# Attention scores over all 128 rows, and the grouped-query keys of x and ctx in one tile

## The chip, the cores and the metric

The kernel runs on one core of one Trainium2 chip. The metric is the device time of one launch in microseconds (us), of which the median of three runs is quoted. TensorE is the engine of the matrix products (PE in the profile, its weight loads PEld), VectorE is DVE, ScalarE is ACT, GpSimd is POOL, and SyncE is SP.

## What is computed

A block with a retention and a recurrent branch is followed by two layers of a second block, all in float32. Each of the two layers mixes three branches: an mLSTM, a grouped-query attention ("gqa") and a neighbourhood attention ("na"). There are 256 tokens of x and 256 tokens of ctx. What matters here are the scores of the two attentions, heads of 64 features each:

```
def attend(q, k, v):                                  # gqa; softmax over all keys
    s = jnp.einsum('bqkgd,bskd->bkgqs', q, k).astype(jnp.float32) * (HEAD_DIM ** -0.5)
    p = jax.nn.softmax(s, axis=-1).astype(v.dtype)
    return jnp.einsum('bkgqs,bskd->bqkgd', p, v)
...
        s_win = jnp.einsum('bqhd,brqjhd->bhqrj', q_row, k_win).astype(jnp.float32) * scale + bias.astype(jnp.float32)
        s_ctx = jnp.einsum('bqhd,bshd->bhqs', q_row, kc).astype(jnp.float32) * scale
        s = jnp.concatenate([s_win.reshape(B, H, GRID_W, wr * wc), s_ctx], axis=-1)
        p = jax.nn.softmax(s, axis=-1).astype(v.dtype)
```

The queries of x see the keys of ctx and of x (512 keys). The queries of ctx, which only the first layer needs, see the keys of ctx alone (256 keys). gqa has 8 query heads on 2 key heads, na has 8 heads.

## The kernel before, in words

**Exact products from two parts.** Every operand of a large product is held as two float32r parts, a high one and a low one (the remainder). `mm3` (lines 120 to 125) makes a product out of three matmuls: high by high, high by low, low by high. These are the lines L123, L124 and L125 in the profile, and nearly all of TensorE's work is there: 128 rows of the contraction, 256 or 512 columns a matmul.

**Scores.** A head has 64 features, so its high and its low part fit one above the other on the 128 partitions. For a query head the tile `aqT` (gqa) or `nq` (na) holds the high part on partitions 0 to 63 and the low part on 64 to 127. For a key head there are two tiles: `akh` (`nkh` in na) holds the high part twice, on both halves; `akl` (`nkl`) holds the low part on partitions 0 to 63 alone. A score is two matmuls into one PSUM bank (a "unit" below has one bank of scores). The first contracts all 128 rows: query high and low with key high. The second contracts 64 rows: query high with key low. These are the lines L838 (gqa) and L925 (na). In gqa the keys of ctx and of x are separate tiles, so a unit of an x query has four matmuls of 256 columns; a unit of ctx queries also has four, two for each of its two tiles of 128 queries. In na the keys of ctx and x lie in one tile, and a unit of x has two matmuls of 512 columns, a unit of ctx four of 256.

**Counts.** A pair is two query heads. Each layer's gqa has four pairs, and each pair has 2 heads times 2 query tiles, so 16 units of x; the first layer has 8 units of ctx beside them. na has the same numbers of units.

**What runs around the scores.** `attend` (from line 629) writes one unit's scores, then lets `fill` trace independent TensorE work (gates L123 to L125, pieces of the modulation L339), then P @ V of a closed pair (L692), then the transposes of the unit two before (L678, L674). The softmax of a unit is VectorE's maximum (L657 or L648), ScalarE's exponential (L659 or L651) and VectorE's scaling (L661 or L653). In na, VectorE also adds the bias to the scores (L928). The list of independent work and the microseconds that are filled in stand in the code; they don't depend on what the change touches. The order on each engine is then made by a scheduler from that trace, and every engine runs its own list in order.

**Making the keys.** gqa: `keys` splits the normed keys token-major in the tile `hs` (high twice on ScalarE L771, low once on VectorE L772), transposes them (L781) and copies them to `akh` and `akl` (L783, L784). This runs once per sequence, at the start of gqa. na: `prepare` makes the queries and keys of one pair with products that are themselves part of the filled-in work, and splits the keys straight out of the PSUM bank `pk`: for each of two heads, ScalarE copies the high part twice (L896) and VectorE subtracts once (L897). It runs four times a layer, one pair ahead of its use, but for the first pair, whose scores wait for it.

**Weights.** Each chunk of 512 KB is loaded by SP into one of four `wr` tiles, cast by ScalarE (L106) and split by VectorE (L107).

Of the kernel before, what the change touches and what calls it, by code (L numbers as in the profile page):

```python
# [23 lines left out]
# microseconds of other TensorE work to trace ahead of the scores of gqa, with each of its units of  # L24
# scores and with each mLSTM head
FILLS = [(8.0, 3.6, 5.0), (4.0, 3.1, 2.5)]
# pieces of the last modulation kept for the gaps of the last layer; of them, those with tiles of their
# own in the layer's pool and in that of its output projection
TAIL, STOCK, STOCK_OUT = 24, 6, 5
# as many of its first pieces for the gap behind the first layer's output projection  # L30
# [30 lines left out]
class Work:  # L61
    """Independent TensorE work: gen(load()) is a generator that traces a piece and yields its microseconds."""
# [10 lines left out]
class Kern:  # L73
# [25 lines left out]
    def weights(self, src, eng=None, into=None):  # L99
        """A chunk [128, n] of weights as two exact float32r parts."""  # L100
# [9 lines left out]
    def split(self, hi, lo, src, scale=None):  # L110
        """hi + lo = src (* scale) as two float32r parts"""
# [8 lines left out]
    def mm3(self, ps, a, b, first, last):  # L120
        """ps (+)= a.T @ b with a, b = (high, low) parts"""
        mm = self.nc.tensor.matmul
        mm(ps, a[0], b[0], start=first, stop=False)  # L123
        mm(ps, a[0], b[1], start=False, stop=False)  # L124
        mm(ps, a[1], b[0], start=False, stop=last)  # L125

    def gemm_pieces(self, w, x, c0, c1, kts=KT, off=0):
        """Feature-major [128 outputs, tokens c0:c1] in pieces; weights stationary."""
# [18 lines left out]
    def gemm_tok(self, src, x, seqs, order=None, eng=None, among=None):  # L147
        """Token-major [128 tokens, 2 tiles, <=256] for each sequence; weights move, four k-tiles a chunk.
        among: (n, f) calls f ahead of the products of the n-th chunk from the end"""
# [19 lines left out]
    def gemm_last(self, src, x):  # L169
        """gemm_tok for one sequence and up to 24 k-tiles, one token tile [128, 256] after the other"""  # L170
# [15 lines left out]
    def step(self):  # L186
        """trace one piece of the independent work that is ready; False where there is none"""
# [17 lines left out]
    def fill(self, us):  # L205
        """trace independent TensorE work of about so many microseconds"""
# [8 lines left out]
    def require(self, works):  # L215
        """trace these pieces of work now, but for those already traced"""
# [6 lines left out]
    def rstd(self, pool, out, ss, n):  # L223
        """out = (ss / n + eps) ** -0.5 by Newton's iteration; its sign changes with each step, and starts negative"""
# [19 lines left out]
    def norm_scale(self, x, pool, ys, junk=None):  # L244
        """ys = rms-normed x, two token tiles; ys may be x where junk is given"""
# [10 lines left out]
    def norm_put(self, ys, temp, hi, lo, c0, gain, shift=None):  # L256
        """hi + lo [128, 8, c0:c0+256] = gain * ys (+ shift), feature-major"""
# [28 lines left out]
    def tanh2(self, out, src):  # L286
        """out = tanh(src / 2) = 2 sigmoid(src) - 1"""
        self.nc.scalar.activation(out, src, AF.Tanh, scale=0.5)

# [17 lines left out]
    def cond(self):  # L307
        """silu of the conditioning vectors, feature-major"""
# [11 lines left out]
    def modulation(self, l, pool=None):  # L320
        """silu(c) @ w_mod + b"""
# [29 lines left out]
    def stock(self, works, pool, n, y=False):  # L351
        """takes n pieces of modulation out of works; tiles of their own (or of the branches' outputs) for their weights"""
# [9 lines left out]
    def fetch(self, works):  # L362
        """their loads behind the last chunk of weights"""
# [5 lines left out]
    def mod_end(self, l, m, row):  # L369
        """one of the six vectors feature-major; gains (1 + scale) g of the norms; rows gate * g of the residual branches to DRAM"""  # L370
# [30 lines left out]
    def first_block(self):  # L401
        nc, A, tc = self.nc, self.A, self.tc
        with ExitStack() as es:
            pa = es.enter_context(tc.tile_pool(name="fa", bufs=1))
            # the parts of both halves of the mixed sequence; before, the LRU's states and ctx
# [5 lines left out]
            # -8 softplus(-lambda) and its half  # L411
# [19 lines left out]
            with tc.issue_after(put):  # L431
                self.cond()
                # half gate biases
# [999 lines left out]
```

## Time and profile before

| | us |
|---|---|
| median of 3 runs | 1889.11 |
| lowest and highest run | 1887.61, 1892.03 |
| profiled execution: span from first to last instruction | 1885.2 |
| PE busy in it | 1816.7 |
| DVE busy in it | 1152.7 |
| ACT busy in it | 861.4 |
| POOL busy in it | 252.9 |

The profile page has no time of the profiled execution but its span; the median run is 3.9 us above it. "Busy" is the time in which at least one instruction of the engine is in progress. The matmuls are pipelined: a matmul that lasts 0.39 us can be followed by the next one after 0.23 us, so what a matmul costs is read from the distance of two starts, not from its duration.

### The profile page before, as it was taken

To read this page: it belongs to the slowest core of one execution; us is meant where nothing else is said; L and a number is where in the kernel's file an instruction comes from. 1 tells how busy PE (TensorE), PEld (TensorE's weight loads), DVE (VectorE), ACT (ScalarE), POOL (GpSimd) and SP (SyncE) were. 2 spreads that over 40 slices of the span, in tenths; PEclk is the share of its full clock that TensorE was granted. 3 is DMA by queue.
4 is the path that set the end of the run, shared out by engine and by line. 5 is a ranking of instruction groups with operands and counts; after the bars stand their busy time and mean duration, and the time that the engine had idled before them with its cause. 6 is when DMAs were issued, how large, how long until landed. Compare 5 with 4: busy or idle time off the path is not lost.

```text
span 1885.2 us, 31900 instructions
## 1 busy us (share of the span) xinstructions
PE 1816.7 (96%) x12484; PEld 1595.4 (85%) x12484; DVE 1152.7 (61%) x2280; ACT 861.4 (46%) x1620; POOL 252.9 (13%) x182
## 2 busy tenths in 40 slices
PE   7998988999999999998999999998999999999998
PEld 6897987666898977787877889998889998779998
DVE  7878768444434667556655564239654448768874
ACT  5463344334435544434444443235555545446653
POOL 2214052000101021004111110021001011002210
PEclk9998998999999999999999999999999999999999
DMA  8853443555524342374354233344444744676563
GB/s 301 282 195 113 138 167 106 184 182 176 193 92 149 88 126 84 101 249 165 113 178 157 96 103 112 107 136 161 151 140 134 239 129 132 196 248 212 185 209 120
DMA packets 114422, 299.33 MB, mean 159 GB/s; under 512 B 28480, under 2 KB 41088, under 8 KB 114016
## 3 DMA queue, kind: packets, MB, share of 16 engines
q1 hardware_dynamic: 113568, 296.37, 47.9%
q8 instruction: 98, 1.61, 0.3%
q0 software_dynamic: 272, 0.36, 0.1%
q10 hardware_dynamic: 432, 0.57, 0.1%
q14 instruction: 52, 0.43, 0.1%
HBM read 281.46 MB, written 19.46 MB: 160 GB/s over the span
## 4 chain that ended last, share of the span: by engine, by line
PE 76%; DVE 6%; ACT 1%; issue 1%; DMA 0%; POOL 0%; DVEq 0%; ACTq 0%; POOLq 0%
PE psg L123 21%; PE psg L124 21%; PE psg L125 20%; PE pss L838 2%; PE psg L692 2%; PE psg L339 2%; PE pst L678 2%; PE pss L925 2%; PE pst L1054 1%; DVE wl L107 1%; PE pss L1042 1%; DVE rstd L240 1%; PE pst L264 0%; ACT wh L106 0%; DVE p L755 0%
## 5 line engine op out<-in xcount | busy, mean ns | idle before, releaser
L107 DVE TENSOR_TENSOR wl<-wr,wh 128x1024 fp32r<-128x1024 f32 x335 | 411.9, 1232 | 328.3 <-ACT wh L106 320.1
L106 ACT CAST wh<-wr 128x1024 fp32r<-128x1024 f32 x370 | 382.4, 1036 | 428.7 <-PE psg L124 182.9
L123 PE MATMUL psg<-hh,wh 128*128 128x256 f32 (+1 forms) x1712 | 577.0, 338 | 0.5 <-ACT hh L279 0.5
L124 PE MATMUL psg<-hl,wh 128*128 128x256 f32 (+1 forms) x1712 | 566.1, 331 | 0.0
L125 PE MATMUL psg<-hh,wl 128*128 128x256 f32 (+1 forms) x1712 | 564.4, 330 | 0.0
L123 PEld LDWEIGHTS psg<-hh,wh 128*128 128x128 f32 x1712 | 327.4, 192 | 54.1 <-issue 16.4
L125 PEld LDWEIGHTS psg<-hh,wl 128*128 128x128 f32 x1712 | 327.8, 192 | 30.2 <-issue 0.8
L124 PEld LDWEIGHTS psg<-hl,wh 128*128 128x128 f32 x1712 | 327.9, 192 | 25.8 <-issue 0.2
L123 PE MATMUL psg<-wh,hh 128*128 128x256 f32 x576 | 165.8, 288 | 6.2 <-DVE p L743 4.3
L125 PE MATMUL psg<-wh,hl 128*128 128x256 f32 x576 | 165.3, 287 | 2.4 <-DVE hl L283 2.4
L124 PE MATMUL psg<-wl,hh 128*128 128x256 f32 x576 | 164.8, 286 | 0.0
L123 PE MATMUL psg<-wh,midh 128*128 128x256 f32 x496 | 140.9, 284 | 0.0
L124 PE MATMUL psg<-wl,midh 128*128 128x256 f32 x496 | 140.9, 284 | 0.0
L125 PE MATMUL psg<-wh,midl 128*128 128x256 f32 x496 | 140.6, 284 | 0.0
L107 POOL TENSOR_TENSOR wl<-wr,wh 128x1024 fp32r<-128x1024 f32 (+1 forms) x35 | 82.5, 2368 | 373.4 <-ACT wh L106 373.4
L1283 POOL TENSOR_TENSOR u<-u 128x512 f32<-128x512 f32 (+1 forms) x44 | 63.3, 1439 | 410.3 <-DVE u L1239 405.3
L123 PEld LDWEIGHTS psg<-wh,hh 128*128 128x128 f32 x576 | 112.1, 195 | 7.1 <-DVE p L743 4.6
L125 PEld LDWEIGHTS psg<-wh,hl 128*128 128x128 f32 x576 | 111.9, 194 | 3.2 <-DVE hl L283 3.2
L124 PEld LDWEIGHTS psg<-wl,hh 128*128 128x128 f32 x576 | 112.0, 195 | 0.1
L123 PEld LDWEIGHTS psg<-wh,midh 128*128 128x128 f32 x496 | 95.6, 193 | 0.0
L124 PEld LDWEIGHTS psg<-wl,midh 128*128 128x128 f32 x496 | 95.6, 193 | 0.0
L125 PEld LDWEIGHTS psg<-wh,midl 128*128 128x128 f32 x496 | 95.6, 193 | 0.0
(300 smaller groups left out, 2915.4 us busy)
## 6 DMA issues: line engine op xcount, KB each, us to landing
wr<-in_w_up_dram SPq DMA_DIRECT2D x88, 512.0 KB, 3.4
wr<-in_w_mod_dram SPq DMA_DIRECT2D x55, 512.0 KB, 3.2
wr<-in_w_zg_dram SPq DMA_DIRECT2D x48, 512.0 KB, 3.5
wr<-in_w_dn_dram SPq DMA_DIRECT2D x45, 512.0 KB, 3.6
wr<-in_w_in_dram SPq DMA_DIRECT2D x40, 512.0 KB, 4.3
wr<-in_w_br_dram SPq DMA_DIRECT2D x24, 512.0 KB, 3.3
wr<-in_w_o_dram SPq DMA_DIRECT2D x20, 512.0 KB, 5.1
stock<-in_w_mod_dram SPq DMA_DIRECT2D x19, 512.0 KB, 6.5
```

The source lines that it names most:

```text
L106: nc.scalar.copy(hi, raw)
L107: self.last_lo = (eng or nc.vector).tensor_tensor(lo, raw, hi.bitcast(F32), ALU.subtract).ins
L123: mm(ps, a[0], b[0], start=first, stop=False)
L124: mm(ps, a[0], b[1], start=False, stop=False)
L125: mm(ps, a[1], b[0], start=False, stop=last)
L240: nc.vector.scalar_tensor_tensor(w[:, c], t[:, c], t[:, c], v[:, c], ALU.mult, ALU.mult)
L339: nc.tensor.matmul(ps[32 * j : 32 * j + 32, 0:T], self.cv[:, kt], raw[j], start=kt == 0, stop=kt == KT - 1)
L678: nc.tensor.transpose(pt[:, k * P : (k + 1) * P], t[:, k * P : (k + 1) * P], self.idn)
L692: nc.tensor.matmul(po[64 * j : 64 * j + 64, :T], p[2](j, k), pTs[id(p), j][:, k], start=k == 0, stop=k == nk - 1)
L838: nc.tensor.matmul(ps[:, i * T : (i + 1) * T], qT[s, pr][: 64 * (2 - c), j, qt * P : (qt + 1) * P], kT[ss, kv][c], start=c == 0, stop=c == 1)
L925: nc.tensor.matmul(ps[:, :n], q[j][: 64 * (2 - c), s * T + qt * P : s * T + (qt + 1) * P], kk[j][c][:, ks], start=c == 0, stop=c == 1)
L1283: nc.gpsimd.tensor_tensor(a, a, b, ALU.mult)
```

## The change

The low parts of the keys are stored on both halves of the partitions, as the high parts were before, so both score matmuls contract all 128 rows. The second one then also multiplies query low by key low, a term that was left out before. In gqa, the keys of ctx and x and both parts go to one tile per key head, `akT`, allocated ahead, so a unit of x has two matmuls of 512 columns instead of four of 256. For this the low part is subtracted twice: in gqa's `hs` (L774 in the changed kernel) and in na's `nkl` (L897), there as copy, subtract, copy, subtract instead of copy, copy, subtract. The two copies out of PSUM for a gqa key head and sequence become one of 512 columns, and the low transposes have 128 columns of output partitions instead of 64.

```
-            kT, vt, qT = {}, {}, {}
+            vt, qT = {}, {}
+            kT = [self.tl(gp, [P, 2, 512], "akT", 2, F32R) for _ in range(2)]
...
                     for c in range(2):
                         nc.scalar.copy(ks[:, :, c], k)
-                    nc.vector.tensor_tensor(ks[:, :, 2], k, ks[:, :, 0].bitcast(F32), ALU.subtract)
+                    for c in range(2):
+                        nc.vector.tensor_tensor(ks[:, :, 2 + c], k, ks[:, :, c].bitcast(F32), ALU.subtract)
...
-                                m = 2 - c
-                                src = ks[:, 2 * tt + kv, 2 * c : 2 * c + m].bitcast(F32).rearrange("p c f -> p (c f)")
-                                nc.tensor.transpose(pt[: 64 * m, c * T + tt * P : c * T + (tt + 1) * P], src, self.idn)
-                        kT[s, kv] = [self.tl(gp, [P, T], "akh", 4, F32R), self.tl(gp, [64, T], "akl", 4, F32R)]
-                        nc.scalar.copy(kT[s, kv][0], pt[:, :T])
-                        nc.scalar.copy(kT[s, kv][1], pt[0:64, T:])
+                                src = ks[:, 2 * tt + kv, 2 * c : 2 * c + 2].bitcast(F32).rearrange("p c f -> p (c f)")
+                                nc.tensor.transpose(pt[:, c * T + tt * P : c * T + (tt + 1) * P], src, self.idn)
+
+                        nc.scalar.copy(kT[kv][:, :, s * T : (s + 1) * T], pt.rearrange("p (c t) -> p c t", c=2))
...
-                    for i, ss in enumerate(ks):
-                        for c in range(2):
-                            nc.tensor.matmul(ps[:, i * T : (i + 1) * T], qT[s, pr][: 64 * (2 - c), j, qt * P : (qt + 1) * P], kT[ss, kv][c], start=c == 0, stop=c == 1)
+                    for c in range(2):
+                        nc.tensor.matmul(ps, qT[s, pr][:, j, qt * P : (qt + 1) * P], kT[kv][:, c, s * T : 512], start=c == 0, stop=c == 1)
...
-                    kl = self.tl(pp, [64, 512], "nkl", 4, F32R)
+                    kl = self.tl(pp, [P, 512], "nkl", 4, F32R)
                     src = pk[64 * j : 64 * j + 64]
                     for c in range(2):
-                        nc.scalar.copy(kh[64 * c : 64 * c + 64], src)
-                    nc.vector.tensor_tensor(kl, src, kh[0:64].bitcast(F32), ALU.subtract)
+                        r = slice(64 * c, 64 * c + 64)
+                        nc.scalar.copy(kh[r], src)
+                        nc.vector.tensor_tensor(kl[r], src, kh[r].bitcast(F32), ALU.subtract)
...
-                        nc.tensor.matmul(ps[:, :n], q[j][: 64 * (2 - c), s * T + qt * P : s * T + (qt + 1) * P], kk[j][c][:, ks], start=c == 0, stop=c == 1)
+                        nc.tensor.matmul(ps[:, :n], q[j][:, s * T + qt * P : s * T + (qt + 1) * P], kk[j][c][:, ks], start=c == 0, stop=c == 1)
```

Where the instructions stand on the engines, before and after (a name's last number tells buffers apart; `psg` is a PSUM bank of products, `pss` of scores, `pst` of transposes, `wh` and `wl` the parts of a weight chunk).

TensorE in the first layer's gqa, one unit of x between gate products, before:

```order
L124 MATMUL psg_3991<-hl_110,wh_3983 128x512
L125 MATMUL psg_3991<-hh_109,wl_3984 128x512
L678 MATMUL pst_3998<-idn,p_3876 128x128 x4
L838 MATMUL pss_4005<-akh_3766,aqT_3850 128x256
L838 MATMUL pss_4005<-akl_3767,aqT_3850 128x256
L838 MATMUL pss_4005<-akh_3512,aqT_3850 128x256
L838 MATMUL pss_4005<-akl_3513,aqT_3850 128x256
L123 MATMUL psg_3991<-hh_109,wh_3983 128x512
```

and now:

```order
L124 MATMUL psg_3977<-hl_110,wh_3969 128x512
L125 MATMUL psg_3977<-hh_109,wl_3970 128x512
L678 MATMUL pst_3984<-idn,p_3868 128x128 x4
L837 MATMUL pss_3991<-akT_3146,aqT_3842 128x512 x2
L123 MATMUL psg_3977<-hh_109,wh_3969 128x512
```

Four score matmuls became two of twice the columns; their neighbours are the same.

ScalarE at the start of the second layer's na, the keys of the first pair (`nkh`), before:

```order
L106 CAST wh_15885<-wr_15883 128x1024
L896 CAST nkh_15749<-psg_15724 64x512 x2
L896 CAST nkh_15754<-psg_15724 64x512 x2
L887 ACTIVATE nq_15818<-psg_15793 64x256
L106 CAST wh_15944<-wr_15942 128x1024
```

and now:

```order
L106 CAST wh_15817<-wr_15815 128x1024
L896 CAST nkh_15677<-psg_15652 64x512 x2
L886 ACTIVATE nq_15748<-psg_15723 64x256
L106 CAST wh_15876<-wr_15874 128x1024
L896 CAST nkh_15683<-psg_15652 64x512
L886 ACTIVATE nq_15751<-psg_15723 64x256
```

The second head's copies, which stood right behind the first head's, now stand behind a weight cast and apart from each other.

VectorE at the same place, before:

```order
L107 TENSOR_TENSOR wl_15886<-wr_15883,wh_15885 128x1024
L897 TENSOR_TENSOR nkl_15750<-psg_15724,nkh_15749 64x512
L928 TENSOR_TENSOR pss_15769<-pss_15769,nbias_15665 128x256
L657 TENSOR_REDUCE sm_15770<-pss_15769 128x1
L897 TENSOR_TENSOR nkl_15755<-psg_15724,nkh_15754 64x512
L658 TENSOR_SCALAR sm_15770<-sm_15770 128x1
```

and now:

```order
L107 TENSOR_TENSOR wl_15818<-wr_15815,wh_15817 128x1024
L897 TENSOR_TENSOR nkl_15678<-psg_15652,nkh_15677 64x512 x2
L887 SCALAR_TENSOR_TENSOR nq_15748<-psg_15723,nq_15748 64x256
L928 TENSOR_TENSOR pss_15699<-pss_15699,nbias_15593 128x256
L107 TENSOR_TENSOR wl_15877<-wr_15874,wh_15876 128x1024
L897 TENSOR_TENSOR nkl_15684<-psg_15652,nkh_15683 64x512
L657 TENSOR_REDUCE sm_15700<-pss_15699 128x1
```

The first unit's maximum (L657) now stands behind two more subtractions, a query split and a weight split.

## Rows read from the trace of the kernel before

**Rows 1.** The page: GB/s in 40 equal slices; the last chain by engine
```profile
GB/s 301 282 195 113 138 167 106 184 182 176 193 92 149 88 126 84 101 249 165 113 178 157 96 103 112 107 136 161 151 140 134 239 129 132 196 248 212 185 209 120
...
PE 76%; DVE 6%; ACT 1%; issue 1%; DMA 0%; POOL 0%; DVEq 0%; ACTq 0%; POOLq 0%
```

**Rows 2.** Windows: length; busy us of PE, PEld, DVE, ACT, POOL; clock, DMA share, GB/s
```profile
295.00:326.00 31.00, 29.64 (x202) 26.00 (x202) 27.02 (x79) 14.69 (x32) 3.39 (x3) 0.94 0.28 94
326.00:455.00 129.00, 129.00 (x749) 88.62 (x749) 55.38 (x121) 46.81 (x100) 0.56 (x1) 1.00 0.54 182
672.00:797.00 125.00, 124.88 (x587) 90.53 (x587) 86.52 (x163) 58.96 (x125) 17.72 (x10) 1.00 0.30 90
1328.00:1415.00 87.00, 87.00 (x631) 75.92 (x630) 50.41 (x94) 45.72 (x92) 0.00 (x0) 1.00 0.43 143
1563.00:1616.00 53.00, 52.76 (x320) 41.61 (x319) 47.48 (x96) 30.38 (x59) 11.70 (x10) 1.00 0.47 139
1616.00:1635.00 19.00, 18.20 (x145) 10.62 (x145) 11.26 (x27) 8.80 (x18) 0.00 (x0) 1.00 0.55 194
```

**Rows 3.** TensorE in order of time: start, duration; a scores unit, first layer's gqa
```profile
335.18 0.39 PE L125 MATMUL psg<-hh,wl 128*128 128x512 f32 x1
335.41 0.28 PE L838 MATMUL pss<-akh,aqT 128*128 128x256 f32 x1
335.62 0.38 PE L838 MATMUL pss<-akl,aqT 64*128 64x256 f32 x1
335.93 0.38 PE L838 MATMUL pss<-akh,aqT 128*128 128x256 f32 x1
336.24 0.38 PE L838 MATMUL pss<-akl,aqT 64*128 64x256 f32 x1
336.55 0.50 PE L123 MATMUL psg<-hh,wh 128*128 128x512 f32 x1
336.89 0.40 PE L124 MATMUL psg<-hl,wh 128*128 128x512 f32 x1
```

**Rows 4.** The same view in the second layer's gqa, two products of 256 columns
```profile
1353.02 0.28 PE L125 MATMUL psg<-hh,wl 128*128 128x256 f32 x1
1353.14 0.28 PE L123 MATMUL psg<-hh,wh 128*128 128x256 f32 x1
```

**Rows 5.** The same view, one pair of score products in the first layer's na
```profile
701.47 0.39 PE L925 MATMUL pss<-nkh,nq 128*128 128x512 f32 x1
701.79 0.50 PE L925 MATMUL pss<-nkl,nq 64*128 64x512 f32 x1
702.22 0.50 PE L123 MATMUL psg<-hh,wh 128*128 128x512 f32 x1
702.55 0.39 PE L124 MATMUL psg<-hl,wh 128*128 128x512 f32 x1
```

**Rows 6.** Groups by shape (count, busy us, mean ns): score products over 64 rows
```profile
L838 PE MATMUL pss<-akl,aqT 64*128 64x256 f32 x80 | 30.2, 380 | 0.0
...
L925 PE MATMUL pss<-nkl,nq 64*128 64x512 f32 x32 | 15.7, 495 | 0.0
...
L925 PE MATMUL pss<-nkl,nq 64*128 64x256 f32 x16 | 6.1, 380 | 0.0
```

**Rows 7.** TensorE in order of time, small transposes over 64 rows each
```profile
516.48 0.22 PE L994 MATMUL pst<-idn,dg 64*128 64x64 f32 x1
516.54 0.22 PE L995 MATMUL pst<-idn,md 64*128 64x64 f32 x1
```

**Rows 8.** The splits by source line (ns min/median/max); who waited for L897 (us, times)
```profile
L772 DVE TENSOR_TENSOR hs<-p,hs x4: 408/414/424, 296.7 to 1328.8; 128x256 fp32r<-128x256 f32 x4
...
L896 ACT CAST nkh<-psg x32: 569/582/585, 672.5 to 1621.4; 64x512 fp32r<-64x512 f32 x32
...
L897 DVE TENSOR_TENSOR nkl<-psg,nkh x16: 671/688/694, 673.8 to 1622.3; 64x512 fp32r<-64x512 f32 x16
...
  ACT nkh L896: 3.6, 3
```


## The prediction

> **What bounds the kernel now.** I read the chain of work first: TensorE holds 76% of it, VectorE 6% [rows 1]. An average says little of the stages that the change touches, so I read busy time next, for the stretches in which the scores stand [rows 2]. In the two gqa stretches TensorE is busy for all of the 129.0 us and all of the 87.0 us, at full clock, while VectorE is busy for 55.4 and 50.4 us. So what TensorE saves there, the kernel saves, if nothing else moves up by as much. The na stretch of the first layer (672 to 797) is also full on TensorE, with VectorE at 86.5 of 125 us. In the second layer's na, from 1563 to 1616, VectorE is busy for 47.5 of 53.0 us beside a full TensorE: two engines near their limit. From 1616 to 1635 VectorE has room again (11.3 of 19 us).
>
> Then I read what a score costs, from starts. In [rows 3] the gate product before the unit and the first score start 0.23 us apart: that is the step of a 512-column matmul in a dense run. [rows 4] gives 0.12 us for 256 columns. Between the scores of the unit, all of 256 columns, the starts lie 0.21, 0.31, 0.31 and 0.31 us apart, and the first gate product behind them takes 0.34 us instead of 0.23. From 335.41 to 336.89 are 1.48 us; without one dense step 1.25 us remain for the unit, where 4 x 0.12 = 0.48 us would do. A score over 128 rows is slow too when it follows one over 64 rows, and so is the gate product behind the unit: it is the passage between 64 and 128 rows that costs, in either direction. [rows 7] supports that: matmuls over 64 rows that follow each other start 0.06 us apart.
>
> **The change part by part, TensorE.** After it no score contracts 64 rows. The counts are from the code and agree with [rows 6]: 80 low products in gqa, 32 of 512 columns and 16 of 256 in na.
>
> - gqa, units of x: 16 in each layer. 1.25 us become two matmuls of 512 columns, 2 x 0.23 = 0.46. Saved 0.79 us x 32 = 25.3 us.
> - gqa, units of ctx: 8, first layer. Four matmuls of 256 columns stay, 1.25 becomes 0.48. Saved 0.77 x 8 = 6.2 us.
> - na, units of x: 32. In [rows 5] a pair takes from 701.47 to 702.55, 1.08 us, less one dense step 0.85; it becomes 0.46. Saved 0.39 x 32 = 12.5 us.
> - na, units of ctx: 8, four matmuls of 256 columns with the steps of [rows 3]. Saved 0.77 x 8 = 6.2 us.
>
> That is 50.2 us. About 8 units are followed by 32-column modulation products, whose passage stays; I take off 0.7 us and have 49.5, of which 31 lie in gqa, 12.4 in the first layer's na and 6.1 in the second's. The wider low transposes cost nothing I can see: there are as many as before.
>
> **What it adds.** *gqa keys.* One more VectorE subtraction of 0.41 us [rows 8] for each sequence, two per layer, in a stage where VectorE is busy for 27.0 of 31 us [rows 2]. The transposes wait for them, and the score tile of x now needs both sequences. Between 0 (other products stand in the gaps) and 4 x 0.41 = 1.6 us: I take 0.8. The single wide copies out of PSUM replace pairs and lie on ScalarE, which has room there: nothing.
>
> *na keys, first pair of each layer.* Its scores wait for the split. Copy, copy, subtract took 0.58 + 0.58 + 0.69 [rows 8]; copy, subtract, copy, subtract takes 2.54, 0.69 more. Bounds 0 and 1.4 for both layers; I take 0.7.
>
> *na keys, the other pairs.* Each pair has two more subtractions, 2 x 0.69 = 1.4 us of VectorE. Copies and subtractions now alternate, and they read one PSUM bank: already before, ScalarE's copies for the second head waited 3 times for the subtraction of the first, 3.6 us in all [rows 8]. So each engine's queue stands while the other works: behind ScalarE's copy are exponentials and weight casts, behind VectorE's subtraction maxima and weight splits, and TensorE waits for both, though one unit or more later. In the first layer VectorE has 86.5 + 5.5 = 92 us of work for a stretch of some 113 us: I take 1.0, bounds 0 and 4. In the second layer, 1563 to 1616, three preparations add 3 x 2 x 0.69 = 4.1 us, so VectorE has 51.6 us of work, while TensorE's 53.0 us shrink by 12 units x 0.39 = 4.7 to 48.3. If the lag runs on into the slack behind 1616, it costs nothing; if VectorE is packed without gaps, 3.3 us; if it keeps its 5.5 us of gaps, the stretch is 57.1 us and the cost 8.8. I take 4.0.
>
> *Weights.* With 17 us saved in the first layer's gqa, its 182 GB/s [rows 2] become 182 x 129/112 = 210 GB/s; the page has slices of 282 and 301 [rows 1]. TensorE waited for no weights there. Nothing.
>
> **The sum.** 49.5 - 0.8 - 0.7 - 1.0 - 4.0 = 43.0 us. The span of 1885.2 becomes 1842.2; with the 3.9 us between the span and the median, 1846. With all costs at zero it is 1839.6; with all at their upper bounds (1.6, 1.4, 4, 8.8) it is 1855.
>
> **The rivals.**
> *B, the alternation in na takes na's gain and more.* For it: VectorE at 90% in the second layer's na, and queues that stand for each other. Against: the preparation runs one pair ahead, and a pair lasts 125/4 = 31 us in the first layer and 72/4 = 18 in the second [rows 2]. Then gqa's 31 us less 1 remain, and na loses up to 5: 1859 to 1864, say 1861.
> *C, the passage isn't what costs; each score product pays for its own weight load.* Then a unit of x has two such steps instead of four, 2 x 0.43 [rows 5] = 0.86 against 1.25, 0.39 x 32 = 12.5 us saved, the rest stays, and 6.5 us of additions come off: 1883. Against it are [rows 7] and the slow gate product behind each unit. Dense gate products all contract the same 128 rows, each with a new weight tile, and keep 0.23 us [rows 3]. The Trainium skill says otherwise ("TensorE: Matmul & The Clock Gate", Part 3, The mechanism): weight loads overlap matmuls in flight only where the row group differs. By that rule the change would put all scores on one row group and hide no load, which is C's time; the dense runs at 0.23 us contradict it.
> *D, the change doesn't do what it says:* something other than TensorE paces gqa, and its units keep their distance. That gives 1889. Against: a TensorE without a gap in both stretches [rows 2].
> *E, slower.* The alternation stands on the path: TensorE runs dry for a whole preparation and its clock falls with it, as in the key stage, where TensorE was idle for 1.4 of 31 us and the granted clock is 0.94 [rows 2]. Price: 4 x (0.58 + 0.69) = 5.1 us for each of 8 preparations, and as much lost to the clock each time as there, 31 x 0.06 = 1.9 us, 56 us against 49.5: 1896. It decides from 6.2 us a preparation; 5.1 us without a clock loss is still faster than before.
>
> **How the numbers follow.** My forecast has 0.82, B 0.12, C 0.03, D 0.01, E 0.02. The likeliest is 1846. Its own range is 1839 to 1855, and I think it holds it 9 times in 10; to leave out no more than 2 in 10 overall the range goes on to B's lower half: 1839 to 1860. A measurement can tell about 0.2%, 3.8 us, from no change. My forecast, B and C are faster by more than that: 0.97. D is the same, 0.01. E is slower, 0.02.
>
> **What would show it.** In the changed profile the scores of gqa (L837) must start 0.23 us apart, those of na (L925) 0.23 or 0.12, and the gate product behind them 0.23 later. The first layer's gqa must shorten by some 17 us, the second's by 12, the first layer's na by 11. If score steps stay above 0.3 us, C is right and the forecast wrong. If they are short but na keeps its length, with TensorE waiting for L928, L896 or L897, it is B. If gqa keeps its length with short steps, look for waits on weights (D). If the granted clock falls below 1 in na, E.

## The result and the profile after

The changed kernel takes 1846.97 us (median of 4 runs, 1845.83 to 1849.25), the kernel before 1888.36 us beside it: the ratio is 0.9782, with a 95% interval of 0.9765 to 0.9799. The forecast was 1846.0, in a range of 1839 to 1860.

The page of the changed kernel: busy time of each engine, and the last chain by engine (to be read against [rows 1]).

```profile
PE 1771.7 (96%) x12420; PEld 1580.4 (86%) x12420; DVE 1162.8 (63%) x2300; ACT 858.6 (47%) x1612; POOL 253.7 (14%) x182
...
PE 73%; DVE 8%; ACT 2%; issue 1%; DMA 0%; POOL 0%; DVEq 0%; ACTq 0%; POOLq 0%
```

TensorE is busy for 45 us less (1816.7 before) and VectorE for 10 us more (1152.7 before), and 3% of the chain has gone from TensorE to VectorE and ScalarE. Where that is, the windows tell: the same stretches as in [rows 2], each moved and shortened by what was gained (length; busy us of PE, PEld, DVE, ACT, POOL; clock, DMA share, GB/s).

```profile
295.00:326.00 31.00, 29.35 (x196) 25.62 (x197) 27.89 (x81) 13.99 (x26) 3.38 (x3) 0.94 0.29 94
326.00:440.00 114.00, 114.00 (x725) 81.72 (x724) 54.45 (x122) 46.95 (x100) 0.56 (x1) 1.00 0.60 205
655.00:768.00 113.00, 112.83 (x590) 89.08 (x591) 90.88 (x171) 58.43 (x125) 16.88 (x10) 1.00 0.33 101
1300.00:1375.00 75.00, 75.00 (x596) 70.24 (x595) 49.51 (x95) 45.06 (x88) 0.00 (x0) 1.00 0.50 166
1523.00:1576.00 53.00, 49.49 (x320) 41.76 (x319) 50.40 (x102) 30.24 (x59) 13.43 (x10) 1.00 0.45 140
1576.00:1596.00 20.00, 17.80 (x150) 11.19 (x150) 12.28 (x28) 8.98 (x18) 0.00 (x0) 1.00 0.51 184
```

Both gqa stretches and the first layer's na are shorter and still full on TensorE. The second layer's na (1523 to 1576) is as long as it was, 53 us: TensorE, which was busy for 52.8 of them, now idles for 3.5, and VectorE is busy for 50.4 instead of 47.5.

TensorE in order of time (start, duration): a scores unit in the first layer's gqa, as in [rows 3], and under it a pair in the first layer's na, as in [rows 5].

```profile
333.83 0.39 PE L125 MATMUL psg<-hh,wl 128*128 128x512 f32 x1
334.06 0.62 PE L837 MATMUL pss<-akT,aqT 128*128 128x512 f32 x2
334.52 0.40 PE L123 MATMUL psg<-hh,wh 128*128 128x512 f32 x1
334.76 0.39 PE L124 MATMUL psg<-hl,wh 128*128 128x512 f32 x1
...
681.27 0.39 PE L125 MATMUL psg<-yh,wl 128*128 128x512 f32 x1
681.50 0.39 PE L925 MATMUL pss<-nkh,nq 128*128 128x512 f32 x1
681.73 0.39 PE L925 MATMUL pss<-nkl,nq 128*128 128x512 f32 x1
681.95 0.39 PE L123 MATMUL psg<-hh,wh 128*128 128x512 f32 x1
```

The two products of the unit take 0.46 us (334.06 to 334.52), and the gate product behind them comes after 0.24. From the gate product ahead (333.83) to the second one behind (334.76) are 0.93 us, where [rows 3] has 1.71 (335.18 to 336.89). The lower four lines are a pair of na, which now has the dense step of 0.23 us throughout, where [rows 5] has 0.32, 0.43 and 0.33.

**Gain by stage.** The products of two traces can be matched one by one: of TensorE's 12228 products that aren't scores, all but 62 have the same shape and the same order in the changed kernel as in the kernel before. The difference of their starts is what a kernel has gained up to there. This table gives, for each stage, the growth of that gain against the profiled run of the kernel before. "Rest" is all that lies outside these stages (before, between and behind them).

| us gained in | gqa 1 with its keys (284 to 486) | na 1 (666 to 808) | gqa 2 with its keys (1297 to 1428) | na 2 (1552 to 1648) | rest | whole span |
|---|---|---|---|---|---|---|
| changed | 17.1 | 12.5 | 11.7 | -0.5 | -1.6 | 39.2 |
| changed_again | 16.5 | 12.5 | 11.7 | -0.6 | -2.7 | 37.4 |
| gqa_only | 18.9 | 0.0 | 11.7 | 0.1 | 1.6 | 32.3 |
| na_only | 0.3 | 12.5 | 0.1 | -0.9 | -2.0 | 10.0 |
| low_adjacent | 5.3 | 0.0 | 5.4 | 0.1 | -2.2 | 8.6 |
| four_products | 15.7 | 12.5 | 11.4 | -0.6 | -2.1 | 36.9 |
| na_grouped | 18.8 | 12.5 | 11.7 | 0.6 | -0.7 | 42.9 |
| na_scalar | 15.8 | 12.5 | 11.7 | 2.7 | 0.4 | 43.1 |
| na_l1_low64 | 17.0 | 12.5 | 11.7 | 0.1 | -3.4 | 37.9 |
| na_extra | 15.8 | 10.1 | 11.8 | -3.5 | -0.4 | 33.8 |
| na_gpsimd | 18.8 | 12.6 | 11.7 | 2.6 | -0.2 | 45.5 |
| keys_scalar | 19.6 | 12.5 | 11.9 | 2.8 | -1.3 | 45.5 |
| keys_scalar_pool | 17.1 | 12.5 | 11.9 | 4.3 | -1.8 | 44.0 |

(1 and 2 are the layers; the times are those of the trace before.) The columns of na 1, gqa 2 and na 2 repeat to 0.1 us wherever the code there is the same, but for the -0.9 of na_only. The first column and the rest don't; why the first doesn't is told in the last section.

### The profile page after: what moved, and what is told of

The parts are those of the page before. It is cut to its first block, busy times and chain, and to the rows that moved or that the text cites. A ratio compares the mean times of both kernels' runs of the same rounds, so it can differ in the third digit from the quotient of the medians.

```text
span 1846.0 us, 31759 instructions
## 1 busy us (share of the span) xinstructions
PE 1771.7 (96%) x12420; PEld 1580.4 (86%) x12420; DVE 1162.8 (63%) x2300; ACT 858.6 (47%) x1612; POOL 253.7 (14%) x182
## 4 chain that ended last, share of the span: by engine, by line
PE 73%; DVE 8%; ACT 2%; issue 1%; DMA 0%; POOL 0%; DVEq 0%; ACTq 0%; POOLq 0%
PE psg L123 21%; PE psg L124 21%; PE psg L125 21%; PE psg L692 2%; PE psg L339 2%; DVE wl L107 1%; PE pst L678 1%; PE pst L1054 1%; PE pss L837 1%; PE pss L1042 1%; PE pss L925 1%; DVE rstd L240 1%; PE pst L264 0%; PE pst L674 0%; DVE nkl L897 0%
```

## Experiments

In each, "changed" is the kernel after the change. Ratios are to the kernel before on the same chip.

### The parts by themselves: gqa_only and na_only

gqa_only keeps the lines of na as they were, na_only those of gqa:

```
 gqa_only:  kl = self.tl(pp, [64, 512], "nkl", 4, F32R)          # and the old split and scores of na
 na_only:   kT[s, kv] = [... "akh" ..., ... "akl" ...]           # and the old keys and scores of gqa
```

> Only gqa is changed (wide key tile, low part on both halves); na keeps its 64-row low products and its splits. Theory (what is saved is TensorE's passage between 64 and 128 rows, 31 us in gqa, less 0.8 for the keys and what else the two stretches lose): the gains of the traces up to here, 17.1 us in the first layer's gqa and 11.7 in the second's, less the 0.9 and 0.5 us lost at the layer's end and before the second key stage, stand by themselves: 1859 to 1861 us. Rival (the parts are not independent; na's gain or the later losses come from gqa's earlier end): outside 1857 to 1864.

> Only na is changed (low part on both halves); gqa keeps its four products a unit. Theory from the trace of the changed kernel: the first layer's na gains 12.5 us and the second's nothing (its TensorE saving of 6.1 us is eaten by VectorE's two more subtractions a pair), so 1888 - 12 = 1876 us, with VectorE saturated and TensorE idle for some 3 us in the second layer's na. Rival (the second layer's na loses its gain only because the faster gqa brings weights or earlier work in another order): then it gains its forecast 2 to 6 us here too, 1870 to 1874.

Measured: gqa_only 1857.25 us (0.9844, 0.9827 to 0.9860), na_only 1877.11 us (0.9945, 0.9930 to 0.9960). The medians are 30.8 and 10.9 us under the 1888.0 beside them, 41.6 together. The changed kernel gained 41.4 (1888.36 less 1846.97). So the parts add up, within the 2 to 3 us by which medians spread. gqa_only came out 2 us under its forecast, in the first layer's gqa (18.9 instead of 17.1). na_only loses 0.9 us in the second layer's na without gqa's help, so gqa's earlier end is not the reason for that loss: the rival for na falls.

### What costs: the passage or the products. low_adjacent and four_products

low_adjacent is the kernel before with another order of the same four products (high, low, low, high), four_products the changed kernel with four products of 256 columns in place of two of 512:

```
 low_adjacent:
-                        for c in range(2):
+                        for c in (i, 1 - i):
                             nc.tensor.matmul(... kT[ss, kv][c], start=c == i, stop=c != i)
 four_products:
-                    for c in range(2):
-                        nc.tensor.matmul(ps, ..., kT[kv][:, c, s * T : 512], ...)
+                    for i, c in [(i, c) for i in range(len(ks)) for c in range(2)]:
+                        nc.tensor.matmul(ps[:, i * T : (i + 1) * T], ..., kT[kv][:, c, ks[i] * T : (ks[i] + 1) * T], ...)
```

> The kernel before, with one edit: in gqa's units of x the four products come as high, low, low, high instead of high, low, high, low, so the two products over 64 rows stand next to each other. Same instructions, same columns, no added VectorE work. Theory (the passage between 64 and 128 rows costs, in either direction, about 0.19 us each): two passages fewer in each of 32 units, the step between the two low products falls from 0.31 to about 0.12 us and one more of the unit with it, 32 x 0.38 = 12 us: 1876. Rival 1 (each product over 64 rows, or each score product with its new weights, costs 0.31 wherever it stands): 1888, steps unchanged. Rival 2 (only the way from 64 up to 128 rows costs): the steps 64 to 128 alone vanish, 32 x 0.19 = 6 us, 1882.

> The changed kernel, but a unit of x in gqa is written with four products of 256 columns over 128 rows instead of two of 512. Theory (the gain is the passage, not the number of products): 4 x 0.12 = 0.48 us a unit against 0.46, 32 x 0.02 = 0.6 us: 1847 to 1848, not to be told from the changed kernel. Rival (a good part of the gain comes from halving the number of products and of weight loads in gqa): 4 products pay 2 steps of 0.2 us or more extra a unit, 32 x 0.2 = 6 us or more: 1853 or more.

Measured: low_adjacent 1878.05 us (0.9947, 0.9931 to 0.9962), four_products 1849.69 us (0.9794, 0.9779 to 0.9809). TensorE in order of time in low_adjacent, the unit that answers to [rows 3]:

```profile
334.12 0.39 PE L125 MATMUL psg<-hh,wl 128*128 128x512 f32 x1
334.34 0.28 PE L838 MATMUL pss<-akh,aqT 128*128 128x256 f32 x1
334.55 0.50 PE L838 MATMUL pss<-akl,aqT 64*128 64x256 f32 x2
334.98 0.39 PE L838 MATMUL pss<-akh,aqT 128*128 128x256 f32 x1
335.21 0.40 PE L123 MATMUL psg<-hh,wh 128*128 128x512 f32 x1
335.44 0.40 PE L124 MATMUL psg<-hl,wh 128*128 128x512 f32 x1
```

From the gate product ahead to the second one behind are 1.32 us (334.12 to 335.44), where [rows 3] has 1.71. So 0.39 us went, by nothing but a new order: two passages of 0.19 us. A product over 64 rows isn't slow in itself: rival 1 would have left 1.71. Rival 2 (only the way up to 128 rows costs) isn't settled by this sum, whatever its forecast of 6 us says: with the whole 0.78 us of a unit on two ways up, one way less would also save 0.39. The single starts settle it. The two low products start at 334.55 and 334.78 (the view puts them on one line). From the first high product to the first low one are 0.21 us and from there to the second low one 0.22, where 0.12 is dense [rows 4]: 0.19 us on the way down. From the second low product to the high one are 0.21, and from there to the gate product 0.23, another 0.2 us on the way up.

The two gqa stages gain 10.7 us (5.3 and 5.4), where 12 were forecast. A unit with the 32-column products of the modulation behind it gains 0.19 instead of 0.39, and five units of x have that, 1.0 us in all.

What a passage holds up, the weight loads (PEld) show. First the kernel before, over the products of [rows 3], then the changed kernel:

```profile
335.18 0.19 PEld L838 LDWEIGHTS pss<-akh,aqT 128*128 128x128 f32 x1
335.61 0.18 PEld L838 LDWEIGHTS pss<-akl,aqT 64*128 64x128 f32 x1 [0.24 <-issue]
...
336.55 0.19 PEld L123 LDWEIGHTS psg<-hh,wh 128*128 128x128 f32 x1
...
334.29 0.19 PEld L123 LDWEIGHTS psg<-hh,wh 128*128 128x128 f32 x1
```

The load of the first score (335.18) starts 0.23 us ahead of its product (335.41), beside the product before it. Behind a change of rows the load starts together with its own product: 335.61 to 335.62 on the way down, 336.55 to 336.55 on the way up. In the changed kernel the gate product's load is 0.23 ahead again (334.29 to 334.52). A load lasts 0.18 to 0.19 us, as much as a passage costs. So rival C of the prediction is half right: a product does wait for its own load, but only where the number of rows changes. That the load is the whole price is read from these traces; no run separates it from anything else that the passage may do.

And the same view of four_products: its unit of four products takes 0.47 us (334.59 to 335.06), the changed kernel's unit of two 0.46.

```profile
334.36 0.39 PE L125 MATMUL psg<-hh,wl 128*128 128x512 f32 x1
334.59 0.63 PE L837 MATMUL pss<-akT,aqT 128*128 128x256 f32 x4
335.06 0.40 PE L123 MATMUL psg<-hh,wh 128*128 128x512 f32 x1
```

Its median is 2.7 us above the changed kernel's, but not through the units: gqa 2 has 11.4 instead of 11.7, and the rest of it lies in the first column and outside the stages, where kernels of the same code differ as much. So the wide key tile's gain is that of its 128 rows. That it also halves the number of score products is worth 0.3 us in the second layer; in the first the column's spread hides it.

### The second layer's na: order, or VectorE's work

Four kernels stood together on one chip: the changed kernel again; na_grouped, with the order copy, copy, subtract, subtract; na_scalar, where ScalarE copies the low part to the other 64 partitions; and na_l1_low64, which in the second layer leaves the low part on 64 partitions.

```
 na_grouped:
                     for c in range(2):
                         nc.scalar.copy(kh[64 * c : 64 * c + 64], src)
+                    for r in (slice(0, 64), slice(64, 128)):
+                        nc.vector.tensor_tensor(kl[r], src, kh[r].bitcast(F32), ALU.subtract)
 na_scalar:
+                    nc.vector.tensor_tensor(kl[0:64], src, kh[0:64].bitcast(F32), ALU.subtract)
+                    nc.scalar.copy(kl[64:128], kl[0:64].bitcast(F32))
 na_l1_low64:
+                    for c in range(2 - l):                      # l is the layer, 0 or 1
+                        nc.vector.tensor_tensor(kl[r], src, kh[r].bitcast(F32), ALU.subtract)
```

> The changed kernel itself, unedited, to stand beside the three variants of its na key split on the same chip. All theories: 1846 to 1848 us, the second layer's na with VectorE busy for some 50 of 53 us.

> The changed kernel, but the na key split is written copy, copy, subtract, subtract instead of copy, subtract, copy, subtract; the same four instructions a head. Theory (in the second layer's na VectorE's sheer work is the bound; 6.6 us of cost there against a saving of 6.1): no change, 1846 to 1848, VectorE still above 0.94 busy there. Rival (the queues standing for each other, ScalarE's copy waiting for VectorE's subtraction, 11.1 us in 12 waits, is what costs): these waits go and 3 to 6 us with them, 1841 to 1844.

> The changed kernel, but the second copy of the low part is made by ScalarE out of SBUF (from the first 64 partitions to the other 64) instead of by a second subtraction of VectorE. Theory (VectorE's work bounds the second layer's na): 3 preparations x 2 x 0.69 = 4.1 us of VectorE go to ScalarE, which is busy for 30 of 53 us there; VectorE's share falls below 0.92, TensorE's waits for p (L659) shrink, and 3 to 6 us come off: 1841 to 1844. Rival (the dependence of VectorE and ScalarE on each other is the cost): the chain copy, copy, subtract, copy is as long as before, no gain, 1846 to 1849.

> The changed kernel, but in the second layer's na the low part of the keys is left on 64 partitions, as before the change (one subtraction a head, 64-row low products); the first layer and gqa are as changed. Theory (the change is worth nothing in the second layer's na: 6.1 us of TensorE saved, 6.6 lost to VectorE): 1846 to 1848, with TensorE busy throughout from 1523 to 1597 instead of VectorE. Rival (the loss has nothing to do with the added subtractions; it would be there with them gone): TensorE's 6.1 us are lost on top, 1852 to 1854.

Measured, beside 1886.75 for the kernel before:

| | median us | ratio | 95% interval |
|---|---|---|---|
| changed_again | 1846.85 | 0.9791 | 0.9777 to 0.9806 |
| na_grouped | 1846.23 | 0.9780 | 0.9763 to 0.9796 |
| na_scalar | 1844.41 | 0.9778 | 0.9762 to 0.9793 |
| na_l1_low64 | 1846.69 | 0.9787 | 0.9771 to 0.9803 |

The medians alone tell none of them apart. The stage does: na 2 gains -0.6, 0.6, 2.7 and 0.1 us. Leaving the change out of the second layer's na costs nothing, as the theory had it. The order by itself brings 1.1 to 1.2 us, VectorE's work (with the order) 3.2 to 3.3.

That the order did what it should, the line of the high copies (nkh) tells. In the changed kernel (ns min/median/max; then how long ScalarE stood before it, and for what):

```profile
L896 ACT CAST nkh<-psg x32: 566/581/586, 655.5 to 1584.6; 64x512 fp32r<-64x512 f32 x32
...
  DVE nkl L897: 11.1, 12
```

And in na_grouped, the line of the subtractions (nkl): who waited for it (us, times).

```profile
L897 DVE TENSOR_TENSOR nkl<-psg,nkh x32: 673/689/695, 653.7 to 1580.7; 64x512 fp32r<-64x512 f32 x32
...
  ACT nkh L895: 2.2, 3
```

ScalarE's 11.1 us of waiting (3.6 before the change, [rows 8]) went down to 2.2. These are both layers together; in the second layer's na alone it was 4.9 us and became 0.4 (ScalarE's waits from 1520 to 1600 in the changed kernel, from 1515 to 1600 in na_grouped):

```profile
ACT nkh L896 <- DVE nkl L897: 4.9, 4, 1.6
...
ACT nkh L895 <- DVE nkl L897: 0.4, 1, 0.4
```

So nearly all of a wait that is plain to see in the profile went, and a quarter of what went (1.1 of 4.5 us) was gained. In the first layer, where the other 4.4 us went, nothing was gained: 12.5 us in both kernels. By its time na_grouped is the theory's "no change"; in the stage it lies between that and the rival's 3 to 6 us. TensorE's own waits from 1520 to 1610 in the changed kernel name what hurt (us in total, times, longest):

```profile
PE pss L925 <- ACT p L659: 2.3, 3, 1.3
PE psg L123 <- DVE fs L1164: 1.4, 1, 1.4
PE psg L692 <- ACT pT L683: 0.7, 1, 0.7
```

By the code the score bank (`pss`) is freed by ScalarE's exponential (L659), which needs VectorE's maximum, which stands in VectorE's queue. In the kernel before, the largest of TensorE's waits in this stretch was 0.6 us.

### The suspected cost doubled, and taken elsewhere

na_extra makes the second subtraction of each head twice. na_gpsimd gives the copy of the low part to GpSimd. keys_scalar is na_scalar with the same copy in the gqa keys. keys_scalar_pool moves, in the second layer, the split of the weights of na's keys to GpSimd as well.

```
 na_extra:
+                    for c, again in ((0, 0), (1, 0), (1, 1)):
+                        r = slice(64 * c, 64 * c + 64)
+                        again or nc.scalar.copy(kh[r], src)
                         nc.vector.tensor_tensor(kl[r], src, kh[r].bitcast(F32), ALU.subtract)
 na_gpsimd:
+                    nc.gpsimd.tensor_copy(kl[64:128], kl[0:64].bitcast(F32))
 keys_scalar:
+                    nc.vector.tensor_tensor(ks[:, :, 2], k, ks[:, :, 0].bitcast(F32), ALU.subtract)
+                    nc.scalar.copy(ks[:, :, 3], ks[:, :, 2].bitcast(F32))
 keys_scalar_pool:
+                    self.weights(A[f"w_nqk{l}"][4 + pr], nc.gpsimd if l else None)
```

> The changed kernel with VectorE's suspected cost doubled: in the na key split the second subtraction of each head is made twice (the repeat writes the same values), so each pair has two more subtractions of 0.69 us on VectorE and nothing else. Theory (VectorE's work bounds the second layer's na, and has room in the first): three preparations x 1.4 = 4.1 us longer there, at most 1 in the first layer: 1850 to 1853. Rival (a subtraction costs wherever it stands, because TensorE or ScalarE waits for it): all 8 preparations pay, 8 x 1.4 = 11 us: 1856 to 1858. Rival 2 (VectorE isn't the bound): 1847, unchanged.

> The changed kernel, but the second copy of the low part of the na keys is made by GpSimd out of SBUF instead of by a second subtraction of VectorE. GpSimd is busy for 13 of the 53 us in question. Theory (VectorE's work is the bound; who takes it over doesn't matter as long as it has room): as with the copy on ScalarE, 1843 to 1846, VectorE below 0.92 busy in the second layer's na. Rival (GpSimd slows VectorE down while it works, or is so slow that the scores wait for nkl): VectorE's subtractions and splits get longer, TensorE waits for L896 to L898, and the time is 1847 or more.

> The changed kernel, with the second copy of the low part made by ScalarE from SBUF in both places: in na as in the run na_scalar, and in the gqa keys (one copy for each sequence in place of VectorE's second subtraction of 0.41 us). Theory (the gqa key stage pays up to 0.41 us for each of 4 added subtractions, na's second layer some 3 us): na_scalar's time less 0 to 1.6 us, 1842 to 1845. Rival (the copy on ScalarE waits for the subtraction, so the chain to the transposes of the keys is as long or longer): 1844 to 1846.

> As keys_scalar, and in the second layer the split of the weights of na's key projection (4 chunks, 1.24 us each on VectorE) is made by GpSimd. Theory (VectorE is still what TensorE waits for in the second layer's na): another 3 x 1.24 = 3.7 us of VectorE gone from a stretch of 51 us with 45.5 of VectorE; TensorE's remaining idle time there, some 1.6 us, shrinks: 1841 to 1844. Rival (GpSimd takes 2.37 us a chunk and the key projection waits for it): 1845 or more.

Measured, beside 1887.31 for the kernel before:

| | median us | ratio | 95% interval |
|---|---|---|---|
| na_extra | 1852.37 | 0.9810 | 0.9794 to 0.9825 |
| na_gpsimd | 1841.93 | 0.9756 | 0.9741 to 0.9771 |
| keys_scalar | 1841.44 | 0.9755 | 0.9740 to 0.9771 |
| keys_scalar_pool | 1843.02 | 0.9768 | 0.9752 to 0.9784 |

The stretch in which TensorE starts the same 320 products of the second layer's na, those of 1563 to 1616 in the kernel before, where it takes 53.00 us [rows 2]: in the changed kernel, na_extra, na_scalar, na_gpsimd and keys_scalar_pool (columns as above; a bound rounded to 0.1 us can drop one product from the count):

```profile
1523.10:1576.20 53.10, 49.59 (x320) 41.85 (x319) 50.30 (x102) 30.14 (x59) 13.43 (x10) 1.00 0.45 139
1524.90:1578.60 53.70, 51.30 (x319) 41.68 (x319) 50.92 (x103) 30.25 (x58) 10.87 (x10) 1.00 0.43 128
1522.20:1572.60 50.40, 48.75 (x320) 41.76 (x319) 45.66 (x96) 34.34 (x65) 11.92 (x10) 1.00 0.48 147
1519.80:1570.70 50.90, 48.64 (x320) 41.77 (x319) 46.34 (x96) 30.52 (x59) 16.62 (x16) 1.00 0.47 145
1523.60:1572.50 48.90, 48.59 (x320) 41.88 (x319) 42.31 (x94) 34.12 (x65) 16.46 (x12) 1.00 0.50 151
```

The first number behind the comma is TensorE, the third VectorE. With VectorE busy for 50.3 us the products take 53.1 us, with 50.9 in na_extra 53.7. With 45.7 and 46.3 they take 50.4 and 50.9, and with 42.3 they take 48.9, and TensorE is full again (48.6). The gain of the whole stage goes the same way: -0.5 for the changed kernel, -3.5, then 2.7, 2.6 and 4.3. So VectorE's work is what bounds this stage, and it doesn't matter whether ScalarE or GpSimd takes it over; GpSimd doesn't hold up VectorE in this place by any amount that the stage shows. One thing moves beside it: the scheduler sets some of TensorE's own products in another order in most of these variants. na_scalar, keys_scalar and keys_scalar_pool have the same order on TensorE in this stage, and between them the gain rises from 2.7 and 2.8 to 4.3 with nothing there but VectorE's weight splits moved.

na_extra lost 2.9 to 3.0 us more than the changed kernel in the second layer's na, where 4.1 were expected, and it missed in another point: it lost 2.4 us in the first layer's na too (10.1 instead of 12.5), where at most 1 was expected. VectorE has 22 of 113 us left there after the change, and 5.5 more don't fill that. But the repeated subtraction isn't all that differs: TensorE's order does too. A pair's P @ V (L692) stands right behind two gate products there, and behind eighteen in the changed kernel, and TensorE waits for VectorE around this place for 0.49 and 0.95 us:

```profile
684.01 1.91 PE L692 MATMUL psg<-pT,nv 128*64 128x256 f32 x14 [0.49 <-DVE pT L681]
688.15 0.50 PE L125 MATMUL psg<-hh,wl 128*128 128x512 f32 x1 [0.95 <-DVE sm L658]
```

So na_extra by itself isn't a clean test. And keys_scalar_pool, the best in its stage, isn't the best as a whole, since its first column is 2.5 us under keys_scalar's. The code there is the same. The copy in the gqa keys is worth 0.2 us in the second layer (11.9 instead of 11.7); in the first, the column's own spread hides it.

na_gpsimd and keys_scalar came 1.1 and 0.6 us under their forecasts, na_scalar 0.4 over its own. na_gpsimd and keys_scalar beat both kernels: their intervals lie below that of changed_again. Against the medians of the changed kernel it is 5 us, of which the traces show 3.1 to 3.4 in the second layer's na; the rest lies in the first column and outside the stages.

## Why the prediction held, step by step

- **The passage between 64 and 128 rows** is what the change saves. Held: low_adjacent takes two passages out of a unit and gains 0.39 us, as 2 x 0.19 says. Rival C, a load paid by every score product, is refuted by the unit of 0.46 us; the loads show that it is paid at a passage. The rule of the Trainium skill that stood beside it ("TensorE: Matmul & The Clock Gate", Part 3, The mechanism: weight loads overlap only where the row group differs) isn't seen here: all score products now use all rows, and keep the dense step. The same section also lets a load go ahead into a background weight buffer, which the prediction left out and the dense steps of 0.23 us agree with.
- **gqa, 31 us, less 0.8 for its keys.** It became 28.8 in the profiled run. The mis-sized term is the 0.7 us for units with modulation products behind them: eight such units of gqa gain some 0.2 us less each (0.58 instead of 0.79 for x), so 1.6. What is left, 31.5 less 1.6 less 28.8, is 1.1 us. About 0.9 of it lies in the second layer, whose units save 12.6 and whose stage gained 11.7: near the 0.8 that was taken for the keys of both layers. In the first layer the stage's own spread hides what the keys cost; gqa_only gained 18.9 us there, more than its units save.
- **na of the first layer, 12.4 less some 1.4.** It became 12.5 in every run that had the change there, but for na_extra with its other order on TensorE: the first pair and the alternation cost nothing.
- **na of the second layer, 6.1 less 4.0 and the first pair's 0.35.** This is the step that failed. It became -0.5: the cost was 6.6. It lies between the 4.0 that I took and the 8.8 of the case in which VectorE keeps its 5.5 us of gaps; it kept 2.6 (53.0 less 50.4). So in this layer alone, rival B is what happened: VectorE takes all that TensorE saves. The added subtractions are only half of it. Of the 6.6 us, 3.2 come back when the second subtraction leaves VectorE (with the order), and another 1.6 with its weight splits, which were there before the change: once TensorE is faster, VectorE's old work paces the stage too. Most of the last 1.8 us lies behind the 320 products: the layer's last four units stand beside 32-column products and brought 0.1 us in keys_scalar_pool, where 4 x 0.39 had been counted.
- **Weights: nothing.** Held: the first layer's gqa ran at 205 GB/s, and TensorE was busy for 114.0 of its 114 us.
- **D and E.** gqa shortened, and the granted clock was 1.00 in both na stretches.
- **The sum.** 43.0 us were forecast, 41.4 came by the medians and 39.2 by the spans. Against the forecast the spans miss 1.4 in gqa, 2.2 in the second layer's na and 1.6 outside the stages, and gain 1.4 in the first layer's na. One step of the working was careless: 3.9 us between span and median were carried over as if fixed. In all runs with a time of their own it is 1.8 us above the span (1847.83 and 1846.0 for the changed kernel). So by that rule the profiled execution of before was one of its faster ones, 2 us under its median, and the changed kernel's was 0.9 over its own. The forecast of 1846.0 was 1.0 us off, with a gain 1.6 us too large and, in the comparison, a kernel before that was 0.75 us faster (1888.36, not 1889.11). That it came so near is luck in part: the misses of 1.4, 2.2 and 1.6 us were made smaller by the 1.4 us of the first layer's na and by the 2.2 us by which the medians' gain is above that of the spans.

## What to carry to other kernels

Price a matmul by the distance of starts, its neighbours included: here a product over fewer rows costs twice, 0.19 us going in and as much coming out, and a change of order alone shows that price cheaply. When TensorE's work is cut by giving another engine more, look at each stage apart: where that engine was at 90% of the stretch, the cut was worth nothing here until work went to engines with room. A large wait between two engines off the critical path (4.9 us here) can be worth 1 us; taking the suspected work away told more than the wait did. And compare a stage between the same products, not between windows of one length.

## What was not expected of the hardware

Kernels with the same code in the first layer's key stage gained between 15.7 and 18.9 us there. VectorE and GpSimd in order of time (start, duration) show where. In the changed kernel, GpSimd's weight split and, in a view of its own, VectorE:

```profile
292.27 2.34 POOL L107 TENSOR_TENSOR wl<-wr,wh 128x1024 fp32r<-128x1024 f32 x1 [2.02 <-ACT wh L106]
```

```profile
292.09 0.16 DVE L235 TENSOR_TENSOR rstd<-rstd,rstd 128x4 f32<-128x4 f32 x1
292.29 2.34 DVE L236 SCALAR_TENSOR_TENSOR hss<-rstd,rstd 128x4 f32<-128x4 f32 x1
294.66 0.49 DVE L743 TENSOR_TENSOR p<-psg,hss 128x128 f32<-128x128 f32 x2
```

The same two views of na_gpsimd:

```profile
292.15 2.38 POOL L107 TENSOR_TENSOR wl<-wr,wh 128x1024 fp32r<-128x1024 f32 x1 [2.17 <-ACT wh L106]
```

```profile
292.02 0.16 DVE L236 SCALAR_TENSOR_TENSOR hss<-rstd,rstd 128x4 f32<-128x4 f32 x1
292.22 0.49 DVE L743 TENSOR_TENSOR p<-psg,hss 128x128 f32<-128x128 f32 x2
292.63 0.68 DVE L736 TENSOR_REDUCE hss<-p 128x8 f32<-128x512 f32 x1
293.22 1.60 DVE L746 TENSOR_TENSOR p<-p,gqk 128x256 f32<-128x256 f32 x1
```

An instruction of VectorE on 4 elements a partition, 0.16 us elsewhere, lasts 2.34 us, as long as GpSimd's split beside it. TensorE waits for the chain that it belongs to: 4.1 us for L743 in the changed kernel, 1.8 in na_gpsimd. In na_gpsimd the split starts when VectorE has got as far as products of PSUM (L743) and a reduction of one input (L736), which keep their usual 0.49 and 0.68 us; it then holds L746, with two inputs in SBUF, which is otherwise 0.41 us, until it ends itself. The Trainium skill has this ("SBUF — State Buffer", Who interferes with whom): an instruction of VectorE with two SBUF inputs contends with one of GpSimd that reads SBUF, for a shared port that is an exclusive lock, and the order of issue decides who waits. The traces agree, 2.34 beside 2.34 us.

The thirteen profiled runs after the change fall into two groups by where this split of GpSimd lands. In gqa_only, na_grouped, na_gpsimd and keys_scalar it holds L746, for 1.5 to 1.6 us, and the stage gains 18.8 to 19.6. In eight others it holds one of the short instructions, for 2.2 to 2.3, as in the kernel before; the seven of them with the changed gqa gain 15.7 to 17.1. In na_only, with the old gqa, it holds L746 as well, and the stage gains only 0.3.

The granted clock settles that case. The stretches ahead of 324.60 and behind it in na_only:

```profile
320.00:324.60 4.60, 3.67 (x22) 2.57 (x21) 2.14 (x4) 3.62 (x6) 0.00 (x0) 1.00 0.43 131
324.60:328.00 3.40, 3.40 (x8) 2.19 (x8) 1.46 (x4) 0.78 (x2) 0.00 (x0) 0.50 0.32 125
```

Behind a stretch in which TensorE idled for 0.9 of 4.6 us, its granted clock is 0.50 from 324.6 to 328.0, the lower of the two levels (1.2 GHz), in the middle of full work: its products start 0.43 us apart instead of 0.23. That takes back 1.5 of the 1.8 us that na_only had gained up to there, as much as gqa_only has over the changed kernel (18.9 less 17.1). In the kernel before and in gqa_only the clock is 1.00 in the same stretch. The clock differs between the groups as well. From 295 to 300 us, in the changed kernel, na_gpsimd and na_scalar (17.1, 18.8 and 15.8 us gained):

```profile
295.00:300.00 5.00, 4.79 (x28) 4.79 (x29) 4.59 (x19) 1.45 (x4) 0.00 (x0) 0.66 0.31 105
295.00:300.00 5.00, 4.31 (x35) 4.08 (x36) 4.59 (x19) 3.24 (x7) 0.00 (x0) 1.00 0.27 105
295.00:300.00 5.00, 5.00 (x25) 5.00 (x25) 4.59 (x20) 1.50 (x5) 0.00 (x0) 0.50 0.04 16
```

So the spread of the first column has two parts, where the split lands and when the clock is low, and no run separates them. Where the split lands follows ScalarE's cast ahead of it. No experiment was made on that: the link between the two groups is read from these traces, not shown by moving the split. The two groups lie 2 to 3 us apart, as much as the two better versions have over na_scalar. Whether one and the same kernel falls into both, no run here shows.
